# Hybrid decoder trunk on one Trainium2 core: the written order of ScalarE and VectorE in the first group of the up projection

## The chip, the cores and the metric

The kernel runs on one core of one Trainium2 chip. The metric is device time of one execution in microseconds; of the kernel before there are three timed runs, and one more execution that the hardware profiler recorded. Names: PE is TensorE, ACT is ScalarE, DVE is VectorE, POOL is GpSimd, SP issues most DMA transfers.

## The reference

One decoder layer on 1024 tokens of width 1024, all in fp32: RMSNorm, a combined input projection, a pooling mixer beside six heads of a gated recurrence, the output projection with a residual, then the MLP and a last RMSNorm. The change lies in the MLP:

```python
    h2 = rms_norm(x, norm_mlp_g[l])
    x = x + jnp.square(jax.nn.relu(h2 @ w_up[l])) @ w_down[l]     # w_up 1024x4096, w_down 4096x1024
```

## The kernel before, in words

Every fp32 operand of a large product is split into two parts (`split`, L114): ACT writes `hi`, a rounded copy; DVE writes `lo = src - hi`. `mm3` (L119) then issues three matmuls: hi by hi (L122), hi by lo (L123), lo by hi (L124). So no product of the MLP starts before ACT and DVE have both touched both of its operands.

The up projection runs in eight groups of 512 columns of `w_up`. Each group is a 2x2 block product by a scheme of seven block products instead of eight. `h2`, the normed and transposed input, lies in four quarters `quad[dk, half]` (half of the 1024 rows of `w_up`, half of the tokens); a group's weights lie in four blocks `raw_wu_{g}_{fh}{dk}`. The token side of product n is `h2op_n`, made once in the first group and used by all eight; the weight side `whi_wu_{g}_n`, `wlo_wu_{g}_n` is made anew in each group. Sums and differences of quarters and blocks (`mixed_blocks` L738, `up_weights` L789: `wsum`, `wdif`) are DVE's.

One product is 24 matmuls of 512 columns into two PSUM banks (e = 0, 1). Products 1, 6, 7 and 4 accumulate one after another in the banks `ps_ua`, 5 and 3 in `ps_uc`, 2 in `ps_ub`. Between two products that share a bank pair the partial sum has to be drained into SBUF (`sums_out` L866): ACT copies it out after products 1, 5 and 6, DVE adds it to an earlier sum after 2, 3 and 7. The next product on that bank waits for the drain. The drains go to tiles `hid` that take the place of quarters no longer needed: the first takes the place of `quad[0,0]`, the source of `h2op_6`, so it waits until both parts of `h2op_6` are made. Finished quarters of the hidden layer are sent to DRAM by POOL's DMA queue (`keep` L863).

The first group runs its products in the order 1, 2, 5, 6, 3, 7, 4 (the others 1, 5, 6, 3, 7, 2, 4). It overlaps the end of the stage before it: the transposes of the last row tile (`mlp_input(7)`, tile `pt_h2_7`) stand on PE between products 1 and 2, and from them ACT and DVE make the last 128 tokens of `h2op_5` and the sources of `h2op_6`, `h2op_3`, `h2op_7` and `h2op_4`.

What sets the order: PE's instructions stand as written. ACT and DVE are ordered by a scheduler, except inside `tc.manual_schedule`, where they stand as written as well. In the kernel before this holds from L829 up to the end of group 0 (L918). In the trace each engine runs its instructions in that order, and what stands behind one that waits is held up with it.

Of the kernel before, what the change touches and what calls it, by code (L numbers as in the profile page):

```python
# [10 lines left out]
F32 = mybir.dt.float32  # L11
F32R = mybir.dt.float32r
# [3 lines left out]
ALU = mybir.AluOpType  # L16
# [44 lines left out]
def kernel(  # L61
# [52 lines left out]
    def split(hi, lo, src):  # L114

        act.copy(hi, src)  # L116
        dve.tensor_tensor(out=lo, in0=src, in1=hi.bitcast(F32), op=ALU.subtract)  # L117
# [540 lines left out]
    def sub(out_, a, b):  # L658
        dve.tensor_tensor(out=out_, in0=a, in1=b, op=ALU.subtract)  # L659
# [11 lines left out]
    with ExitStack() as pb:  # L671
# [63 lines left out]
            h2[n] = pair_of(pool_, f"h2op_{n}")  # L735
            split(*h2[n], src)

        def mixed_blocks(i):  # L738


            b11, b12, b21, b22 = (quad[k][:, :, i % 4 * P:(i % 4 + 1) * P] for k in ((0, 0), (0, 1), (1, 0), (1, 1)))
            sub(b11, b12, b11)
            sub(b12, b22, b12)
            split(*(t[:, :, i % 4 * P:(i % 4 + 1) * P] for t in h2[5]), b11)
            sub(b11, b22, b11)
            sub(b21, b21, b11)

        def product_out(step, dh):
# [37 lines left out]
            nc.sync.dma_start(t, w_up_v[:, 4 * dk:4 * dk + 4, c0:c0 + 256])  # L786
            return t

        def up_weights(g, n, w, s):  # L789

            if n == 5:
                s[0] = sums.tile([P, 4, 256], F32, tag="sum", name=f"wsum_{g}")
                add(s[0], w[1, 0], w[1, 1])
            elif n == 6:
                sub(s[0], s[0], w[0, 0])
            elif n == 3:
                sub(s[0], w[0, 1], s[0])
            elif n == 7:
                s[1] = sums.tile([P, 4, 256], F32, tag="sum", name=f"wdif_{g}")
                sub(s[1], w[0, 0], w[1, 0])  # L800
            src = {1: w[0, 0], 2: w[0, 1], 3: s.get(0), 4: w.get((1, 1)), 5: s.get(0), 6: s.get(0), 7: s.get(1)}[n]
            pool_ = wring["split"][0]
            hi = pool_.tile([P, 4, 256], F32R, tag="whi", name=f"whi_wu_{g}_{n}")
            lo = pool_.tile([P, 4, 256], F32R, tag="wlo", name=f"wlo_wu_{g}_{n}")
            split(hi, lo, src)
            return hi, lo

# [18 lines left out]
            w_first[fh, dk] = up_raw(0, fh, dk, pool_)  # L826
        for n in (1, 2, 5):
            split_first[n] = up_weights(0, n, w_first, s_first)
        steady = tc.manual_schedule(engines={mybir.EngineType.DVE, mybir.EngineType.Activation})  # L829
        steady.__enter__()  # L830
        for n, key in ((1, "a"), (2, "b")):
            first[key] = up_banks(0, key)
            for _ in up_product(n, split_first[n], first[key], True):
                pass
            if n == 1:
                split_first[6] = up_weights(0, 6, w_first, s_first)
                mlp_input(7)
                mixed_blocks(7)

        later = {6: (big, quad[0, 0]), 3: (big, quad[1, 1]), 7: (big2, quad[0, 1]), 4: (big2, quad[1, 0])}  # L840

        def up_group(g, order):
            if g:
                w = {(fh, dk): up_raw(g, fh, dk, pool_) for fh, dk, pool_ in ((0, 0, wraw), (0, 1, wraw), (1, 0, rawp), (1, 1, rawp))}
                banks, s, ready = {}, {}, {}
            else:
                w, banks, s, ready = w_first, dict(first), s_first, split_first
# [30 lines left out]
                    if e:  # L878
                        relu2(c[q])

            for at_, n in enumerate(order):
                key = {1: "a", 6: "a", 7: "a", 4: "a", 5: "c", 3: "c", 2: "b"}[n]
                if g == 0:
                    for m in order[3:at_ + 3] or order[3:4]:
                        if m in later:
                            operand(m, *later.pop(m))
                            if m not in ready:
                                ready[m] = up_weights(g, m, w, s)
                if g == 0 and n in (1, 2):
                    for e in range(2):  # L890
                        sums_out(n, e, banks[key][e])
                else:
                    fresh = key not in banks
                    if fresh:
                        banks[key] = up_banks(g, key)
                    weights = ready[n] if n in ready else up_weights(g, n, w, s)
                    for e in up_product(n, weights, banks[key], fresh):
                        sums_out(n, e, banks[key][e])
                if n in (2, 7, 4):
                    keep({2: 1, 7: 4, 4: 2}[n], c[{2: 11, 7: 22, 4: 21}[n]])  # L900
                if n == order[-2]:

                    s3 = quarter("hs3")
                    sub(s3, c[11], c[12])
                    keep(7, s3)
                    add(c[12], c[12], c[22])
                    keep(5, c[12])
                    s2 = quarter("hs2")
                    sub(s2, c[12], c[11])
                    keep(6, s2)  # L910
# [3 lines left out]

        for g in range(UP_GROUPS):
            up_group(g, ORDER if g else FIRST_ORDER)
            if g == 0:
                steady.__exit__(None, None, None)  # L918
    quadp.release()
    sums.release()  # L920
    rawp.release()
# [178 lines left out]
```

## Time and profile before

| | us |
|---|---|
| median of 3 runs | 1112.06 (1111.24 to 1114.28) |
| the profiled execution | 1111.47 |
| its span, first to last instruction | 1109.7 |
| PE busy in the span | 1084.5 (98%) |
| DVE busy | 792.5 (71%) |
| ACT busy | 422.2 (38%) |

The span is divided into 40 slices of 27.7 us. Shares of busy time are means over stages that have different limits; matmuls are pipelined, so a busy PE counts a slow matmul as busy too. PEclk is the clock granted to TensorE, 1.00 or 9 tenths and more being 2.4 GHz and half of it 1.2 GHz; a mean in between says that part of the stretch ran at either. In a timeline a row is one instruction or several equal ones; what stands in brackets is the engine's idle time before it and what ended that.

### The profile page before, as it was taken

The numbers are of one execution on the slowest core, as the hardware profiler recorded it, in microseconds if no ns is written. First come the engines' busy times: TensorE is split into PE (matmuls) and PEld (weight loads), VectorE is DVE, ScalarE is ACT, GpSimd is POOL, SyncE is SP. The second block draws the span as 40 slices with busy tenths as digits, with TensorE's granted clock in tenths as the row PEclk, the third lists the DMA queues.
The fourth block names the chain that finished last, engine by engine and source line by source line (L and its number), as shares of the span: only waits on it lengthen the run. The fifth ranks groups of instructions, "written<-read, shape, count | busy, mean of one in ns | idle before, by whom it ended". The sixth has DMA issues, their size and how long they took to land.

```text
span 1109.7 us, 14274 instructions
## 1 busy us (share of the span) xinstructions
PE 1084.5 (98%) x5728; PEld 896.0 (81%) x5728; DVE 792.5 (71%) x1068; ACT 422.2 (38%) x647; POOL 81.9 (7%) x124
## 2 busy tenths in 40 slices
PE   8989999999999999997999999999999999999996
PEld 6868797879787788876888888888888888888885
DVE  4398847784779852688678558756988978777774
ACT  6744333434332522344332233233344424233343
POOL 1001010101010111100010011001000000000001
PEclk9999999999999999998999999999999999999998
DMA  9421011110110162313544354336994344344104
GB/s 318 148 58 38 21 39 38 39 39 20 58 39 19 58 218 95 105 39 108 176 177 146 114 190 171 133 114 221 368 354 185 124 180 161 113 164 177 38 1 152
DMA packets 71362, 137.55 MB, mean 124 GB/s; under 512 B 4864, under 2 KB 44928, under 8 KB 67712
## 3 DMA queue, kind: packets, MB, share of 16 engines
q1 hardware_dynamic: 60656, 100.98, 26.8%
q0 software_dynamic: 9344, 33.56, 7.8%
q10 hardware_dynamic: 1296, 2.10, 0.5%
q8 instruction: 45, 0.74, 0.3%
q14 instruction: 21, 0.17, 0.0%
HBM read 98.87 MB, written 37.75 MB: 123 GB/s over the span
## 4 chain that ended last, share of the span: by engine, by line
PE 80%; DVE 11%; issue 3%; ACT 3%; DMA 2%; POOL 1%; SPq 0%; ACTq 0%; POOLq 0%; DVEq 0%
PE ps_dx L123 5%; PE ps_dx L124 5%; PE ps_dx L122 5%; PE ps_ua L122 5%; PE ps_ua L124 5%; PE ps_ua L123 5%; PE ps_dy L123 3%; PE ps_dy L124 3%; PE ps_dy L122 3%; PE ps_uc L124 2%; PE ps_uc L122 2%; PE ps_uc L123 2%; PE ps_o L122 2%; PE ps_o L124 2%; PE ps_o L123 2%
## 5 line engine op out<-in xcount | busy, mean ns | idle before, releaser
L116 ACT CAST wdop<-raw_wd 128x2048 fp32r<-128x2048 f32 x28 | 53.6, 1913 | 155.6 <-PE ps_dy L124 49.1
L122 PE MATMUL ps_ua<-h2op,whi_wu 128*128 128x512 f32 x256 | 100.5, 393 | 3.9 <-DVE hid L662 3.8
L124 PE MATMUL ps_ua<-h2op,wlo_wu 128*128 128x512 f32 x256 | 100.5, 392 | 0.0
L123 PE MATMUL ps_ua<-h2op,whi_wu 128*128 128x512 f32 x256 | 100.2, 392 | 0.0
L122 PE MATMUL ps_dx<-wdop,hop 128*128 128x512 f32 x256 | 99.6, 389 | 0.0
L123 PE MATMUL ps_dx<-wdop,hop 128*128 128x512 f32 x256 | 99.6, 389 | 0.0
L124 PE MATMUL ps_dx<-wdop,hop 128*128 128x512 f32 x256 | 99.6, 389 | 0.0
L117 DVE TENSOR_TENSOR wdop<-raw_wd,wdop 128x2048 fp32r<-128x2048 f32 x28 | 64.1, 2290 | 28.7 <-ACT wdop L116 28.7
L117 DVE TENSOR_TENSOR wlo_wu<-raw_wu,whi_wu 128x1024 fp32r<-128x1024 f32 x24 | 29.2, 1222 | 52.9 <-ACT whi_wu L116 52.9
L117 DVE TENSOR_TENSOR hop<-hraw,hop 128x2048 fp32r<-128x2048 f32 x28 | 64.0, 2284 | 3.4 <-ACT hop L116 3.4
L116 ACT CAST hop<-hraw 128x2048 fp32r<-128x2048 f32 x28 | 53.4, 1910 | 32.1 <-DMA hraw<-hid 20.8
L116 ACT CAST whi_wu<-wsum 128x1024 fp32r<-128x1024 f32 x24 | 25.3, 1053 | 96.7 <-DVE wsum L659 41.2
L122 PEld LDWEIGHTS ps_ua<-h2op,whi_wu 128*128 128x128 f32 x256 | 48.5, 189 | 14.7 <-issue 4.2
L662 DVE TENSOR_TENSOR x<-ps_dx,x 128x512 f32<-128x512 f32 x64 | 43.9, 688 | 20.3 <-PE ps_dx L124 20.3
L124 PEld LDWEIGHTS ps_ua<-h2op,wlo_wu 128*128 128x128 f32 x256 | 48.4, 189 | 10.5 <-DVE wlo_wu L117 0.4
L123 PEld LDWEIGHTS ps_ua<-h2op,whi_wu 128*128 128x128 f32 x256 | 48.5, 189 | 10.2
L122 PE MATMUL ps_v<-whi_v,hT_hi 128*128 128x256 f32 x192 | 54.5, 285 | 1.8 <-ACT whi_v L116 1.8
L122 PEld LDWEIGHTS ps_dx<-wdop,hop 128*128 128x128 f32 x256 | 48.1, 188 | 10.0
L123 PEld LDWEIGHTS ps_dx<-wdop,hop 128*128 128x128 f32 x256 | 48.1, 188 | 9.9
L124 PEld LDWEIGHTS ps_dx<-wdop,hop 128*128 128x128 f32 x256 | 48.1, 188 | 9.9
L123 PE MATMUL ps_v<-wlo_v,hT_hi 128*128 128x256 f32 x192 | 54.3, 284 | 0.8 <-DVE wlo_v L117 0.8
L124 PE MATMUL ps_v<-whi_v,hT_lo 128*128 128x256 f32 x192 | 54.1, 284 | 0.0
(234 smaller groups left out, 2781.2 us busy)
## 6 DMA issues: line engine op xcount, KB each, us to landing
hid<-hid POOLq DMA_DIRECT2D x56, 512.0 KB, 3.1
hraw<-hid SPq DMA_DIRECT2D x28, 1024.0 KB, 5.0
raw_wu<-in_w_up_dram SPq DMA_DIRECT2D x32, 512.0 KB, 3.7
raw_wd<-in_w_down_dram SPq DMA_DIRECT2D x16, 1024.0 KB, 7.1
xt<-in_x_t_dram SPq DMA_DIRECT2D x8, 512.0 KB, 7.5
xn<-in_x_dram SPq DMA_DIRECT2D x8, 512.0 KB, 6.9
x<-x_mid SPq DMA_DIRECT2D x8, 512.0 KB, 6.0
raw_v<-in_w_in_dram SPq DMA_DIRECT2D x6, 512.0 KB, 3.9
```

What stands on the lines that cost most here:

```text
L116: act.copy(hi, src)
L117: dve.tensor_tensor(out=lo, in0=src, in1=hi.bitcast(F32), op=ALU.subtract)
L122: pe.matmul(ps, lh, rh, start=start, stop=False, skip_group_check=goes_on)
L123: pe.matmul(ps, lh, rl, start=False, stop=False, skip_group_check=goes_on)
L124: pe.matmul(ps, ll, rh, start=False, stop=stop, skip_group_check=goes_on)
L662: dve.tensor_tensor(out=out_, in0=a, in1=b, op=ALU.add)
```

## The change

Only group 0 is written anew; the groups after it keep their code, and PE keeps its order. `split` is taken apart into `hi_part` (ACT) and `lo_part` (DVE), and the two are written at different places. The manual order now begins before the bank pair of product 1 is taken and ends after the operands of product 4, so the drains of 3, 7 and 4 in group 0 are placed by the scheduler.

```diff
--- before.py
+++ after.py
@@ -735,14 +735,23 @@
             h2[n] = pair_of(pool_, f"h2op_{n}")
             split(*h2[n], src)
 
-        def mixed_blocks(i):
+        def hi_part(hi, lo, src):
+            act.copy(hi, src)
+
+        def lo_part(hi, lo, src):
+            dve.tensor_tensor(out=lo, in0=src, in1=hi.bitcast(F32), op=ALU.subtract)
+
+        def mixed_blocks(i, between=lambda: None):
 
 
             b11, b12, b21, b22 = (quad[k][:, :, i % 4 * P:(i % 4 + 1) * P] for k in ((0, 0), (0, 1), (1, 0), (1, 1)))
             sub(b11, b12, b11)
+            part = *(t[:, :, i % 4 * P:(i % 4 + 1) * P] for t in h2[5]), b11
+            hi_part(*part)
+            between()
+            lo_part(*part)
+            sub(b11, b22, b11)
             sub(b12, b22, b12)
-            split(*(t[:, :, i % 4 * P:(i % 4 + 1) * P] for t in h2[5]), b11)
-            sub(b11, b22, b11)
             sub(b21, b21, b11)
 
         def product_out(step, dh):
@@ -786,7 +795,7 @@
             nc.sync.dma_start(t, w_up_v[:, 4 * dk:4 * dk + 4, c0:c0 + 256])
             return t
 
-        def up_weights(g, n, w, s):
+        def up_sum(g, n, w, s):
 
             if n == 5:
                 s[0] = sums.tile([P, 4, 256], F32, tag="sum", name=f"wsum_{g}")
@@ -798,10 +807,15 @@
             elif n == 7:
                 s[1] = sums.tile([P, 4, 256], F32, tag="sum", name=f"wdif_{g}")
                 sub(s[1], w[0, 0], w[1, 0])
-            src = {1: w[0, 0], 2: w[0, 1], 3: s.get(0), 4: w.get((1, 1)), 5: s.get(0), 6: s.get(0), 7: s.get(1)}[n]
+            return {1: w[0, 0], 2: w[0, 1], 3: s.get(0), 4: w.get((1, 1)), 5: s.get(0), 6: s.get(0), 7: s.get(1)}[n]
+
+        def up_split(g, n):
             pool_ = wring["split"][0]
-            hi = pool_.tile([P, 4, 256], F32R, tag="whi", name=f"whi_wu_{g}_{n}")
-            lo = pool_.tile([P, 4, 256], F32R, tag="wlo", name=f"wlo_wu_{g}_{n}")
+            return tuple(pool_.tile([P, 4, 256], F32R, tag=f"w{part}", name=f"w{part}_wu_{g}_{n}") for part in ("hi", "lo"))
+
+        def up_weights(g, n, w, s):
+            src = up_sum(g, n, w, s)
+            hi, lo = up_split(g, n)
             split(hi, lo, src)
             return hi, lo
 
@@ -826,20 +840,40 @@
             w_first[fh, dk] = up_raw(0, fh, dk, pool_)
         for n in (1, 2, 5):
             split_first[n] = up_weights(0, n, w_first, s_first)
-        steady = tc.manual_schedule(engines={mybir.EngineType.DVE, mybir.EngineType.Activation})
-        steady.__enter__()
-        for n, key in ((1, "a"), (2, "b")):
-            first[key] = up_banks(0, key)
-            for _ in up_product(n, split_first[n], first[key], True):
-                pass
-            if n == 1:
-                split_first[6] = up_weights(0, 6, w_first, s_first)
-                mlp_input(7)
-                mixed_blocks(7)
-
-        later = {6: (big, quad[0, 0]), 3: (big, quad[1, 1]), 7: (big2, quad[0, 1]), 4: (big2, quad[1, 0])}
+        places_first = {6: (big, quad[0, 0]), 3: (big, quad[1, 1]), 7: (big2, quad[0, 1]), 4: (big2, quad[1, 0])}
+
+        def first_operand(n):
+            pool_, src = places_first[n]
+            h2[n] = pair_of(pool_, f"h2op_{n}")
+            return *h2[n], src
+
+        def first_weights(n):
+            src = up_sum(0, n, w_first, s_first)
+            split_first[n] = up_split(0, n)
+            return *split_first[n], src
+
+
+        in_order = tc.manual_schedule(engines={mybir.EngineType.DVE, mybir.EngineType.Activation})
+        in_order.__enter__()
+        first["a"] = up_banks(0, "a")
+        for _ in up_product(1, split_first[1], first["a"], True):
+            pass
+        mlp_input(7)
+        made = {}
+        mixed_blocks(7, lambda: made.update({6: first_weights(6)}))
+        made["op6"] = first_operand(6)
+        hi_part(*made[6])
+        hi_part(*made["op6"])
+        lo_part(*made[6])
+        lo_part(*made["op6"])
+        made["op3"] = first_operand(3)
+        hi_part(*made["op3"])
+        first["b"] = up_banks(0, "b")
+        for _ in up_product(2, split_first[2], first["b"], True):
+            pass
 
         def up_group(g, order):
+
             if g:
                 w = {(fh, dk): up_raw(g, fh, dk, pool_) for fh, dk, pool_ in ((0, 0, wraw), (0, 1, wraw), (1, 0, rawp), (1, 1, rawp))}
                 banks, s, ready = {}, {}, {}
@@ -878,24 +912,46 @@
                     if e:
                         relu2(c[q])
 
-            for at_, n in enumerate(order):
-                key = {1: "a", 6: "a", 7: "a", 4: "a", 5: "c", 3: "c", 2: "b"}[n]
-                if g == 0:
-                    for m in order[3:at_ + 3] or order[3:4]:
-                        if m in later:
-                            operand(m, *later.pop(m))
-                            if m not in ready:
-                                ready[m] = up_weights(g, m, w, s)
-                if g == 0 and n in (1, 2):
-                    for e in range(2):
-                        sums_out(n, e, banks[key][e])
-                else:
-                    fresh = key not in banks
-                    if fresh:
-                        banks[key] = up_banks(g, key)
-                    weights = ready[n] if n in ready else up_weights(g, n, w, s)
-                    for e in up_product(n, weights, banks[key], fresh):
-                        sums_out(n, e, banks[key][e])
+            def drain(n):
+                for e in range(2):
+                    sums_out(n, e, banks[bank_of[n]][e])
+
+            def run(n):
+                key = bank_of[n]
+                fresh = key not in banks
+                if fresh:
+                    banks[key] = up_banks(g, key)
+                weights = ready[n] if n in ready else up_weights(g, n, w, s)
+                return up_product(n, weights, banks[key], fresh)
+
+            bank_of = {1: "a", 6: "a", 7: "a", 4: "a", 5: "c", 3: "c", 2: "b"}
+            if g == 0:
+                drain(1)
+                made[3] = first_weights(3)
+                lo_part(*made["op3"])
+                for e in run(5):
+                    sums_out(5, e, banks["c"][e])
+                hi_part(*made[3])
+                lo_part(*made[3])
+                made["op7"] = first_operand(7)
+                hi_part(*made["op7"])
+                made[7] = first_weights(7)
+                hi_part(*made[7])
+                drain(2)
+                keep(1, c[11])
+                for e in run(6):
+                    sums_out(6, e, banks["a"][e])
+                lo_part(*made["op7"])
+                lo_part(*made[7])
+                made["op4"], made[4] = first_operand(4), first_weights(4)
+                for part in (hi_part, lo_part):
+                    part(*made["op4"])
+                    part(*made[4])
+                in_order.__exit__(None, None, None)
+                order = order[4:]
+            for n in order:
+                for e in run(n):
+                    sums_out(n, e, banks[bank_of[n]][e])
                 if n in (2, 7, 4):
                     keep({2: 1, 7: 4, 4: 2}[n], c[{2: 11, 7: 22, 4: 21}[n]])
                 if n == order[-2]:
@@ -914,8 +970,6 @@
 
         for g in range(UP_GROUPS):
             up_group(g, ORDER if g else FIRST_ORDER)
-            if g == 0:
-                steady.__exit__(None, None, None)
     quadp.release()
     sums.release()
     rawp.release()
```

ACT, around the last transposes. `quad` rows are the copies of the transposed tile, `h2op` and `whi_wu` are `hi` parts (`whi_wu_0_6` is group 0, product 6), `hid` rows are drains. Before:

```order
L116 CAST whi_wu_0_5_4391<-wsum_0_4389 128x1024
L116 CAST whi_wu_0_6_4424<-wsum_0_4389 128x1024
L730 COPY quad_01_3700<-pt_h2_7_0_4428 128x4x128
L730 COPY quad_11_3703<-pt_h2_7_1_4434 128x4x128
L116 CAST h2op_5_4179<-quad_00_3702 128x4x128
L116 CAST h2op_6_4472<-quad_00_3702 128x2048
L872 COPY hid_0_0_4475<-ps_ua_0_0_4397 128x512
L872 COPY hid_0_0_4475<-ps_ua_0_1_4398 128x512
L116 CAST h2op_3_4482<-quad_11_3703 128x2048
L116 CAST whi_wu_0_3_4486<-wsum_0_4389 128x1024
```

After:

```order
L116 CAST whi_wu_0_5_4391<-wsum_0_4389 128x1024
L730 COPY quad_01_3700<-pt_h2_7_0_4423 128x4x128
L730 COPY quad_11_3703<-pt_h2_7_1_4429 128x4x128
L739 CAST h2op_5_4179<-quad_00_3702 128x4x128
L739 CAST whi_wu_0_6_4438<-wsum_0_4389 128x1024
L739 CAST h2op_6_4444<-quad_00_3702 128x2048
L739 CAST h2op_3_4449<-quad_11_3703 128x2048
L906 COPY hid_0_0_4477<-ps_ua_0_0_4397 128x512
L906 COPY hid_0_0_4477<-ps_ua_0_1_4398 128x512
L906 COPY hid_0_0_4477<-ps_uc_0_0_4484 128x512
L906 COPY hid_0_0_4477<-ps_uc_0_1_4485 128x512
L739 CAST whi_wu_0_3_4481<-wsum_0_4389 128x1024
```

The two copies of the transposes and the last part of `h2op_5` now stand ahead of `whi_wu_0_6`; `h2op_3` stands ahead of the drain of product 1; and the drain of product 5 stands ahead of `whi_wu_0_3`.

DVE, from the `lo` part of `h2op_6` to that of product 7's weights (`ps_ub` is product 2's drain, the row behind its two is the squared ReLU). Before:

```order
L117 TENSOR_TENSOR h2op_6_4472<-quad_00_3702,h2op_6_4472 128x2048
L662 TENSOR_TENSOR hid_0_0_4475<-ps_ub_0_0_4446,hid_0_0_4475 128x512
L662 TENSOR_TENSOR hid_0_0_4475<-ps_ub_0_1_4447,hid_0_0_4475 128x512
L861 SCALAR_TENSOR_TENSOR hid_0_0_4475<-hid_0_0_4475 128x1024
L117 TENSOR_TENSOR h2op_3_4482<-quad_11_3703,h2op_3_4482 128x2048
L659 TENSOR_TENSOR wsum_0_4389<-raw_wu_0_01_4375,wsum_0_4389 128x1024
L117 TENSOR_TENSOR wlo_wu_0_3_4487<-wsum_0_4389,whi_wu_0_3_4486 128x1024
L117 TENSOR_TENSOR h2op_7_4518<-quad_01_3700,h2op_7_4518 128x2048
L659 TENSOR_TENSOR wdif_0_4521<-raw_wu_0_00_4373,raw_wu_0_10_4377 128x1024
L117 TENSOR_TENSOR wlo_wu_0_7_4524<-wdif_0_4521,whi_wu_0_7_4523 128x1024
```

After:

```order
L742 TENSOR_TENSOR h2op_6_4444<-quad_00_3702,h2op_6_4444 128x2048
L659 TENSOR_TENSOR wsum_0_4389<-raw_wu_0_01_4375,wsum_0_4389 128x1024
L742 TENSOR_TENSOR h2op_3_4449<-quad_11_3703,h2op_3_4449 128x2048
L742 TENSOR_TENSOR wlo_wu_0_3_4482<-wsum_0_4389,whi_wu_0_3_4481 128x1024
L659 TENSOR_TENSOR wdif_0_4516<-raw_wu_0_00_4373,raw_wu_0_10_4377 128x1024
L662 TENSOR_TENSOR hid_0_0_4477<-ps_ub_0_0_4451,hid_0_0_4477 128x512
L662 TENSOR_TENSOR hid_0_0_4477<-ps_ub_0_1_4452,hid_0_0_4477 128x512
L895 SCALAR_TENSOR_TENSOR hid_0_0_4477<-hid_0_0_4477 128x1024
L742 TENSOR_TENSOR h2op_7_4514<-quad_01_3700,h2op_7_4514 128x2048
L742 TENSOR_TENSOR wlo_wu_0_7_4519<-wdif_0_4516,whi_wu_0_7_4518 128x1024
```

The three rows of product 2's drain stood directly behind `h2op_6` and stand now behind the operands of product 3.

DVE, from the operands of product 4 to the drain of product 7 (`ps_ua`); `ps_uc` is the drain of product 3, `wlo_wu_1_1` belongs to group 1. Before:

```order
L117 TENSOR_TENSOR h2op_4_4554<-quad_10_3701,h2op_4_4554 128x2048
L117 TENSOR_TENSOR wlo_wu_0_4_4558<-raw_wu_0_11_4379,whi_wu_0_4_4557 128x1024
L662 TENSOR_TENSOR hid_0_1_4539<-ps_uc_0_0_4490,hid_0_1_4539 128x512
L662 TENSOR_TENSOR hid_0_1_4539<-ps_uc_0_1_4491,hid_0_1_4539 128x512
L117 TENSOR_TENSOR wlo_wu_1_1_4667<-raw_wu_1_00_4656,whi_wu_1_1_4666 128x1024
L861 SCALAR_TENSOR_TENSOR hid_0_1_4539<-hid_0_1_4539 128x1024
L662 TENSOR_TENSOR hid_0_0_4475<-ps_ua_0_0_4397,hid_0_0_4475 128x512
L662 TENSOR_TENSOR hid_0_0_4475<-ps_ua_0_1_4398,hid_0_0_4475 128x512
```

After:

```order
L742 TENSOR_TENSOR h2op_4_4554<-quad_10_3701,h2op_4_4554 128x2048
L742 TENSOR_TENSOR wlo_wu_0_4_4556<-raw_wu_0_11_4379,whi_wu_0_4_4555 128x1024
L662 TENSOR_TENSOR hid_0_1_4537<-ps_uc_0_0_4484,hid_0_1_4537 128x512
L662 TENSOR_TENSOR hid_0_1_4537<-ps_uc_0_1_4485,hid_0_1_4537 128x512
L662 TENSOR_TENSOR hid_0_0_4477<-ps_ua_0_0_4397,hid_0_0_4477 128x512
L895 SCALAR_TENSOR_TENSOR hid_0_1_4537<-hid_0_1_4537 128x1024
L117 TENSOR_TENSOR wlo_wu_1_1_4667<-raw_wu_1_00_4656,whi_wu_1_1_4666 128x1024
L662 TENSOR_TENSOR hid_0_0_4477<-ps_ua_0_1_4398,hid_0_0_4477 128x512
```

The first half of product 7's drain moved up by two rows, ahead of the squared ReLU and `wlo_wu_1_1`; its second half stands behind them.

## Rows read from the trace of the kernel before

**Rows 1.** The page: busy time of each engine; granted clock in 40 slices.

```profile
PE 1084.5 (98%) x5728; PEld 896.0 (81%) x5728; DVE 792.5 (71%) x1068; ACT 422.2 (38%) x647; POOL 81.9 (7%) x124
...
PEclk9999999999999999998999999999999999999998
```

**Rows 2.** Busy time by stretch; columns in the first line.

```profile
core 0: us, PE busy (x) PEld busy (x) DVE busy (x) ACT busy (x) POOL busy (x), PEclk, DMA share, GB/s
478.50:529.20 50.70, 44.37 (x180) 34.26 (x178) 41.94 (x44) 21.78 (x26) 3.33 (x6) 0.93 0.26 88
529.20:567.30 38.10, 38.10 (x170) 31.56 (x169) 28.01 (x29) 12.03 (x15) 3.19 (x6) 1.00 0.49 166
490.60:497.30 6.70, 6.05 (x24) 4.42 (x24) 4.73 (x6) 2.84 (x4) 0.00 (x0) 1.00 0.00 0
504.80:512.30 7.50, 7.45 (x24) 5.67 (x25) 4.83 (x4) 4.00 (x5) 0.00 (x0) 0.77 0.26 70
522.00:529.20 7.20, 7.17 (x25) 5.75 (x25) 7.20 (x7) 1.64 (x2) 1.60 (x3) 0.76 0.37 146
```

**Rows 3.** Timeline of PE in group 0: start, us, instruction [idle before, releaser].

```profile
484.08 1.03 PE L728 MATMUL pt_h<-ident,hn 128*128 128x128 f32 x8
484.87 0.48 PE L122 MATMUL ps_ub<-h2op,whi_wu 128*128 128x512 f32 x1
...
490.96 0.50 PE L122 MATMUL ps_uc<-h2op,whi_wu 128*128 128x512 f32 x1 [0.39 <-ACT h2op L116]
...
497.32 0.50 PE L122 MATMUL ps_ua<-h2op,whi_wu 128*128 128x512 f32 x1
...
504.80 0.50 PE L122 MATMUL ps_uc<-h2op,whi_wu 128*128 128x512 f32 x1 [1.75 <-ACT hid L872]
...
508.32 0.63 PE L122 MATMUL ps_uc<-h2op,whi_wu 128*128 128x512 f32 x1
...
512.35 0.39 PE L122 MATMUL ps_ua<-h2op,whi_wu 128*128 128x512 f32 x1
...
522.03 0.47 PE L122 MATMUL ps_ua<-h2op,whi_wu 128*128 128x512 f32 x1 [3.83 <-DVE hid L662]
...
529.20 0.39 PE L122 MATMUL ps_ua<-h2op,whi_wu 128*128 128x512 f32 x1
```

**Rows 4.** Timeline of ACT in group 0.

```profile
487.34 1.05 ACT L116 CAST whi_wu<-wsum 128x1024 fp32r<-128x1024 f32 x1 [4.80 <-DVE wsum L659]
488.30 1.07 ACT L730 COPY quad<-pt_h 128x512 f32<-128x512 f32 x2
...
492.41 1.91 ACT L116 CAST h2op<-quad 128x2048 fp32r<-128x2048 f32 x1 [1.50 <-DVE quad L659]
496.68 1.07 ACT L872 COPY hid<-ps_ua 128x512 f32<-128x512 f32 x2 [2.36 <-DVE h2op L117]
...
504.17 1.07 ACT L872 COPY hid<-ps_uc 128x512 f32<-128x512 f32 x2
```

**Rows 5.** Timeline of DVE in group 0.

```profile
483.09 0.69 DVE L659 TENSOR_TENSOR quad<-quad,quad 128x512 f32<-128x512 f32 x1
...
504.30 1.23 DVE L117 TENSOR_TENSOR wlo_wu<-wsum,whi_wu 128x1024 fp32r<-128x1024 f32 x1 [1.11 <-ACT whi_wu L116]
507.07 2.29 DVE L117 TENSOR_TENSOR h2op<-quad,h2op 128x2048 fp32r<-128x2048 f32 x1 [1.55 <-ACT h2op L116]
...
517.74 1.28 DVE L662 TENSOR_TENSOR hid<-ps_uc,hid 128x512 f32<-128x512 f32 x2
518.93 1.22 DVE L117 TENSOR_TENSOR wlo_wu<-raw_wu,whi_wu 128x1024 fp32r<-128x1024 f32 x1
520.06 1.22 DVE L861 SCALAR_TENSOR_TENSOR hid<-hid 128x1024 f32<-128x1024 f32 x1
521.20 1.28 DVE L662 TENSOR_TENSOR hid<-ps_ua,hid 128x512 f32<-128x512 f32 x2
```

**Rows 6.** Instructions of the tiles `hid`, 515 to 540 us: landing of their DMAs.

```profile
DMA to landing us min/median/max: 2.9/2.9/3.3
```

## Prediction, made before the changed kernel was run

> **What bounds the kernel now.** I read the page first: PE is busy 98% of the span, DVE 71%, ACT 38%, and the granted clock is full in every slice but the nineteenth and the last [rows 1]. The last is the end of the kernel. The nineteenth, 18 x 27.7 = 499 to 527 us, lies in group 0 of the up projection. Then a table by stretch: group 0 takes 50.70 us from the start of product 1 (478.50) to the start of group 1, and group 1, with the same 168 matmuls, takes 38.10 with PE busy in all of it [rows 2]. So a product at full pace is 38.10/7 = 5.44 us. Group 0 has eight transposes besides (484.08 to 484.87, 0.79 us [rows 3]) and product 1, which also starts behind transposes, takes 484.08 - 478.50 = 5.58, 0.14 over the pace; I allow product 2 another 0.1. Without a wait the group would take 38.10 + 0.79 + 0.24 = 39.13. The rest, 50.70 - 39.13 = 11.57 us, is what any better order of ACT and DVE can win here. I found no other wait of PE worth a term.
>
> Where the 11.57 lie, product by product, from the starts in [rows 3]. Product 2 starts at 484.87 and ends its matmuls near 490.41 (5.44 + 0.1).
> - Product 5 starts at 490.96 and product 6 at 497.32 instead of 490.41 + 5.44 = 495.85: 1.47 lost.
> - Product 3 starts at 504.80 instead of 497.32 + 5.44 = 502.76: 2.04 lost, behind ACT's drain of product 5.
> - Product 3 runs 7.55 us up to 512.35 instead of 5.44: 2.11 lost. The stretch 504.80 to 512.30 has a granted clock of 0.77 [rows 2], so part of it at 1.2 instead of 2.4 GHz; a matmul there lasts 0.63 us instead of 0.39 [rows 3]. PE had idled 1.75 us just before.
> - Product 7 takes 9.68 us up to 522.03 with the wait behind it, 3.83 of them idle: 4.24 lost, waiting for DVE to take product 7 out of its bank.
> - Product 4 runs 7.17 instead of 5.44, clock 0.76: 1.73 lost, again after idling.
> Sum 11.59. The waits make 7.75 of it and the low clock behind the two longest 3.84.
>
> The cause stands in the rows of ACT and DVE. ACT idles 4.80 us before `whi_wu` of product 6, and behind it both copies of the transposes wait although PE made them at 484.08; they go out at 488.30 [rows 3, 4]. All of DVE's work on the last tile follows from these copies. From there ACT and DVE hand each other one operand at a time: ACT waits 1.50 and 2.36 [rows 4], DVE 1.55 for an `h2op` [rows 5]. At the end DVE writes the drain of product 3, `wlo_wu` of group 1 and the ReLU (517.74 to 521.20) before it takes up product 7, which PE had finished near 518 [rows 3, 5].
>
> **The change part by part.** No instruction is added or removed, PE's order stays, and no DMA is issued from a new place in the program; two spills on POOL's queue swap places, and so do two loads of group 2 on SP's. I walk the new order with durations of the trace. On DVE a 512-wide row is followed after 0.60, a 1024-wide one after 1.13, a 2048-wide one after its 2.29 less the same overlap, 2.20 [rows 5]; a result counts 0.09 later. On ACT these steps are 0.49, 0.96 and 1.82 [rows 4]. DVE's first moved instruction starts at 483.09, as before.
> - Copies first. ACT is free at 482.5 (487.34 - 4.80), the first four transposes end near 484.7, so the copies end near 485.8 instead of 489.4: 3.6 earlier. DVE comes to the last tile's difference after four 0.60 steps and one 1.13 at 486.6, it ends at 487.3; ACT's part of `h2op_5` ends at 488.0; DVE's, behind the 1.13 of `wsum`, at 489.1. Product 5 is due at 490.41: 1.3 in hand, its wait is gone.
> - Product 6. Three differences, the `lo` of its weights and of `h2op_6` follow: 3 x 0.60 + 1.13 + 2.20 after 489.0, ended at 494.3; ACT's `hi` of `h2op_6`, which starts behind the first difference, ends at 491.7, just ahead of DVE. ACT's two drains of product 1 wait for that and end at 494.9 and 495.4; due 495.85 and 498.6. 0.9 in hand.
> - Product 3. `wsum`, `h2op_3` (ACT made its `hi` ahead, by 493.6) and `wlo` take 1.13 + 2.20 + 1.13, so up to 498.8. ACT's four drains end when product 5 does, near 496.7, and its `whi` at 497.7, just as DVE wants it. Due 501.3: over 2 in hand. This is the 2.04 wait and, with it, the slow clock behind it.
> - Product 7. `wdif`, product 2's drain (1.19 + 1.13 [rows 5]), `h2op_7`, `wlo`: 1.13 + 2.32 + 2.20 + 1.13 brings DVE to 505.7. Due 506.7 for its first matmul and 0.45 later for `wlo`: some 1.2 in hand. The drain behind the splits costs nothing, for only the spill of that quarter waits for it.
> - Product 4. Its operands end at 509.1, product 3's drain at 510.3, the first half of product 7's at 510.9; PE finishes product 7 at 512.2. The second half, behind ReLU and `wlo_wu_1_1`, ends at 513.8 and is due at 514.9. The 3.83 wait and its slow clock are gone too.
> - What is late next: `wlo` of group 1's product 5. DVE never rests from 483.09 on, and this row now stands behind six 1024-wide and two 512-wide rows: it ends near 523.0, and is due at 523.06 + 0.45 = 523.5. 0.5 in hand, the smallest margin. After it DVE has less to do (28.01 of 38.10 in group 1 [rows 2]) and catches up.
>
> So all 11.57 goes, if DVE keeps its pace. The trace has no stretch in which DVE works 40 us without rest; the nearest is 522.0 to 529.2, busy 7.20 of 7.20 [rows 2]. Bounds: its rows there keep their 1.13 step, which gives no loss; if every instruction that uses the result of the one just before it paid 0.14 more, as many as four on this way make 0.56, at most 0.1 beyond the margin. A wait that small doesn't touch the clock: the stretch with the 0.39 wait before product 5 has 1.00 [rows 2, 3]. A gain above 11.57 is excluded, since group 1's pace is PE's floor. I take 11.6.
>
> One rule speaks against an unbroken DVE. The spills of the hidden layer are issued by POOL, and they must land before group 1's drains can reuse the tiles; they landed in 2.9 to 3.3 us [rows 6] although DVE was busy without a pause in 522.0 to 529.2, where three of them were issued. The Trainium skill (GPSIMD Engine Reference, section Specifications) says that GpSimd's SBUF interfaces are shared with VectorE, with contention against instructions with two SBUF inputs, which nearly all of these are. By that rule the spill of the second quarter, ready near 516, would stall until DVE rests, and the gain would be that of the second rival below; by the row it is 11.6.
>
> **The rivals.**
> - Part of the waits comes back elsewhere. For it: margins of 0.5 and 0.9, and a chain of 39 DVE rows in which one late ACT part shifts all. Against it: each step was made with durations that vary by hundredths. A wait of 0.5 to 1.5 without a change of clock gives 11.6 - 1 = 10.6; one like 1.75 with the clock behind it costs 2.0 + 2.1 = 4.1, so 7.5.
> - The spills stall until DVE rests. That is two 1024-wide rows behind the last one above, 525.3; landed at 525.3 + 3.0 = 528.3, ACT's drain of group 1's product 1 and behind it `whi` of product 6 end near 530.5, due 528.5: 2 us and 2 of clock, gain 7.6. The landing time in [rows 6] speaks against it.
> - The waits aren't made by the order. If drains were slow for another reason, copies that come earlier would only wait longer, and PE would keep the 2.04 and 4.24 and the clock behind them: gain 1.5 at most. Against it: the two long waits end within 0.15 us of the first half of the drain that is named, ACT's at 504.17 + 0.58 and DVE's at 521.20 + 0.69 [rows 3 to 5].
> - Slower: DVE becomes the bound. In the new order ACT and DVE work side by side for 40 us. Were DVE's rows longer for that, each per cent would be 0.4 us; PE starts to wait at 1%, and together with two falls of the clock (3.8) the kernel is slower than before from (11.6 - 3.8)/0.4 = 20%; at 25% it is 2 us slower, 1114. Against it: a 1024-wide row beside a working ACT (504.30) takes 1.23, two beside an idle one (518.93, 520.06) 1.22 [rows 5].
>
> **How the numbers follow.** The profiled execution took 1111.47, which is 1.77 around a span of 1109.7; outside group 0 only a few rows of ACT and DVE in group 1 swap places, so it becomes 1111.47 - 11.6 = 1099.9. The median of the runs lies 0.59 above it: 1112.06 - 11.6 = 1100.5. Chances: forecast 0.76; waits in part elsewhere 0.15 (1101.5 to 1104.6); spills 0.02 (1104.5); order not the cause 0.04 (1110.5); slower 0.03. The range goes from the lowest run shown less the gain and a little spread, 1099.0, to a full new wait with its clock, 1104.6. No change means within 0.3%, 3.3 us, about what a measurement of this kernel can resolve: the first three cases are faster, 0.93; the fourth is the same, 0.04; the last slower, 0.03.
>
> **What would show it.** In the profile after: group 0 from product 1 to group 1 in 39.1 to 39.6 us, clock 1.00 in all of it, no wait of PE above 0.5; the copies of `pt_h` on ACT near 484.7; DVE busy over 95% from 483 to 523; the slice with 8 in the clock row gone. I am wrong if PE still waits for a drain in `ps_ua` or `ps_uc`, if group 1 shows waits that it didn't have, or if group 0 is short and the stages behind it are longer by what it saved.

## The result, and the profile after

The changed kernel takes 1100.26 us (median of 4 runs, 1098.87 to 1101.15), the kernel before 1111.65 beside it (4 runs, 1110.69 to 1114.28): ratio 0.9893, 95% interval 0.9873 to 0.9913. The forecast was 1100.5 in a range of 1099.0 to 1104.6.

The page of the profile after: busy times, and the granted clock in 40 slices.

```profile
PE 1079.2 (98%) x5728; PEld 894.1 (81%) x5728; DVE 791.8 (72%) x1068; ACT 422.0 (38%) x647; POOL 81.9 (7%) x124
...
PEclk9999999999999999999999999999999999999998
```

The counts of instructions are those of [rows 1], and the 8 in the nineteenth slice is gone. The table by stretch, group 0 and then group 1, with the columns of [rows 2]:

```profile
478.82:517.93 39.11, 39.11 (x180) 32.46 (x178) 38.28 (x42) 20.64 (x25) 2.81 (x5) 1.00 0.31 101
517.93:556.01 38.08, 38.08 (x170) 31.54 (x168) 30.81 (x31) 13.03 (x17) 3.72 (x7) 1.00 0.53 179
```

Group 0 takes 39.11 us instead of 50.70, with PE busy in all of it at full clock; group 1 keeps its pace. The span fell from 1109.7 to 1098.4, by 11.3, and group 0 by 11.59: all of the gain is here, and the rest of the kernel is 0.3 longer. The starts of the transposes and of products 2, 5, 6, 3, 7, 4 and then of group 1, on PE after:

```profile
484.40 1.03 PE L728 MATMUL pt_h<-ident,hn 128*128 128x128 f32 x8
485.19 0.48 PE L122 MATMUL ps_ub<-h2op,whi_wu 128*128 128x512 f32 x1
...
490.73 0.39 PE L122 MATMUL ps_uc<-h2op,whi_wu 128*128 128x512 f32 x1
...
496.17 0.39 PE L122 MATMUL ps_ua<-h2op,whi_wu 128*128 128x512 f32 x1
...
501.61 0.39 PE L122 MATMUL ps_uc<-h2op,whi_wu 128*128 128x512 f32 x1
...
507.05 0.39 PE L122 MATMUL ps_ua<-h2op,whi_wu 128*128 128x512 f32 x1
...
512.49 0.39 PE L122 MATMUL ps_ua<-h2op,whi_wu 128*128 128x512 f32 x1
...
517.93 0.39 PE L122 MATMUL ps_ua<-h2op,whi_wu 128*128 128x512 f32 x1
```

No row has a wait, and the steps are 5.44 us from product 5 on. The three waits and the slow matmul of [rows 3] are gone. ACT after, where [rows 4] had the wait of 4.80:

```profile
485.04 1.07 ACT L730 COPY quad<-pt_h 128x512 f32<-128x512 f32 x2 [2.16 <-PE pt_h L728]
...
490.15 3.73 ACT L739 CAST h2op<-quad 128x2048 fp32r<-128x2048 f32 x2 [0.27 <-DVE quad L659]
494.70 1.08 ACT L906 COPY hid<-ps_ua 128x512 f32<-128x512 f32 x2 [0.81 <-DVE h2op L742]
495.66 1.30 ACT L906 COPY hid<-ps_uc 128x512 f32<-128x512 f32 x2
496.85 1.05 ACT L739 CAST whi_wu<-wsum 128x1024 fp32r<-128x1024 f32 x1
```

The copies wait for PE's transposes alone, two `h2op` his follow each other (x2), and both drains of product 5 come ahead of `whi` of product 3. DVE after, the rows that the walk dated:

```profile
497.93 1.22 DVE L742 TENSOR_TENSOR wlo_wu<-wsum,whi_wu 128x1024 fp32r<-128x1024 f32 x1
...
504.87 1.22 DVE L742 TENSOR_TENSOR wlo_wu<-wdif,whi_wu 128x1024 fp32r<-128x1024 f32 x1
...
513.41 0.68 DVE L662 TENSOR_TENSOR hid<-ps_ua,hid 128x512 f32<-128x512 f32 x1
...
522.02 1.22 DVE L117 TENSOR_TENSOR wlo_wu<-wsum,whi_wu 128x1024 fp32r<-128x1024 f32 x1
```

They end at 499.15, 506.09, 514.09 and 523.24; the walk had 498.8, 505.7, 513.8 and 523.0. Group 0 also started 0.32 later than before (478.82 against 478.50), so each step is within 0.1 of its forecast.

### The profile page after: what moved, and what is told of

Read it like the earlier page. It is cut to its first block, busy times and chain, and to the rows that moved or that the text cites. A ratio compares the mean times of both kernels' runs of the same rounds, so it can differ in the third digit from the quotient of the medians.

```text
span 1098.4 us, 14269 instructions
## 1 busy us (share of the span) xinstructions
PE 1079.2 (98%) x5728; PEld 894.1 (81%) x5728; DVE 791.8 (72%) x1068; ACT 422.0 (38%) x647; POOL 81.9 (7%) x124
## 4 chain that ended last, share of the span: by engine, by line
PE 85%; DVE 8%; issue 2%; DMA 2%; ACT 2%; POOL 1%; SPq 0%; ACTq 0%; POOLq 0%
PE ps_dx L123 5%; PE ps_ua L124 5%; PE ps_ua L122 5%; PE ps_dx L124 5%; PE ps_dx L122 5%; PE ps_ua L123 5%; PE ps_o L122 3%; PE ps_dy L123 3%; PE ps_uc L124 3%; PE ps_uc L122 3%; PE ps_dy L124 3%; PE ps_dy L122 3%; PE ps_uc L123 3%; PE ps_o L123 3%; PE ps_o L124 3%
```

## Experiments: undoing one part, doing one part

The forecast walked the whole order. It did not show which part carries the gain. Times compare by the ratio to the kernel before in the same series, and by group 0's length in the profile, from product 1's start to group 1's: 50.70 before, 39.11 after.

**Copies late again.** On ACT and DVE, against the changed kernel:

```
+        made = {6: first_weights(6)}
+        hi_part(*made[6])
         mlp_input(7)
-        made = {}
-        mixed_blocks(7, lambda: made.update({6: first_weights(6)}))
+        lo_part(*made[6])
+        mixed_blocks(7)
...
```

> The changed kernel, but the two copies of the last transposes stand behind whi of product 6 on ACT again (and wlo of product 6 ahead of the last tile's differences on DVE). My theory, that PE waits where a row of ACT or DVE ends later than PE wants it, and that the parts of the change each keep a margin: product 5 waits 1.0 to 1.6 us and product 6 another 1.0, nothing behind them; group 0 takes 41.7 instead of 39.1 us, the kernel 1102.9; if the clock falls behind the first wait, up to 2 more, 1104.9. Rival, that this one place was the cause and the rest follows from it: the waits before products 3 and 4 come back with their low clock, 1108 to 1111.

1102.25 us, ratio 0.9917 (0.9904 to 0.9931). PE waits 1.06 and 0.22 in product 5, which starts 1.2 late; product 6 comes another 0.9 late, and the profile marks no wait behind that. Group 0 takes 41.32, 2.2 more than after, clock 1.00. The first theory holds, with 0.4 less than it said. The waits before products 3, 7 and 4 don't come back, so late copies alone don't make them.

**Product 2's drain at once.** `drain(2)` moves from behind the splits to right behind `drain(1)`.

> The changed kernel, but DVE's drain of product 2 (two additions and the ReLU, 2.3 us) stands right behind ACT's drain of product 1, ahead of the splits for products 3 and 7. My theory: product 7 alone waits, 0.8 us, since the drain holds DVE until PE has finished product 2; the kernel takes 1101.1. Rival, that drains ahead of splits were the main cause of the waits: a wait of over 2 us and a low clock behind it, 1104 or more.

1100.60 us, ratio 0.9903 (0.9889 to 0.9916): not to be told from the changed kernel. Group 0 takes 39.55, product 7 starts 0.44 late. The expected reason was wrong: PE had long finished product 2, and DVE waits 0.65 for ACT's copy of product 1 into the same `hid`.

**ACT's lead taken away, in part.** `hi` of `h2op_3` goes behind `drain(1)`, `hi_part(*made[3])` ahead of the drain of product 5.

> The changed kernel, but ACT is not one operand ahead: the hi part of h2op_3 stands behind the drain of product 1, and whi of product 3 ahead of the drain of product 5. My theory: DVE waits about 1.5 us for h2op_3 once and this reaches PE only before product 4, 1.2 us; the kernel takes 1101.5. Rival, that ACT one operand ahead is what breaks the hand-over of pairs: waits before products 3 and 4 both, 1104 to 1108. Second rival, copies first alone was enough: no wait, 1100.3.

1100.71 us, ratio 0.9906 (0.9892 to 0.9921). Group 0 takes 39.92, 0.8 more; the wait (0.34, for `wlo`) shows in product 7, not before product 4. I first read this as: the lead is worth little. It was not fully taken away, though, since the sum for product 3's weights still stood ahead of the `lo` of `h2op_3`.

**Copies first alone.** The kernel before with the copies first; in the same run the sum of product 6's weights (`between`, in `mixed_blocks`) stands behind all of the last tile's differences, where the change has it between the two parts of `h2op_5`:

```
             sub(b21, b21, b11)
+            between()
...
             if n == 1:
-                split_first[6] = up_weights(0, 6, w_first, s_first)
                 mlp_input(7)
-                mixed_blocks(7)
+                mixed_blocks(7, lambda: split_first.update({6: up_weights(0, 6, w_first, s_first)}))
```

> The kernel before, with one part of the change alone: the copies of the last transposes stand ahead of whi of product 6 on ACT, and wlo of product 6 behind the last tile's differences on DVE. My theory: the wait before product 5 goes, but ACT and DVE still hand each other one operand at a time and DVE still drains product 3 ahead of product 7; products 6, 3, 7 and 4 start where they did within 1 us, group 0 takes 50 to 51 us, the kernel 1111 to 1112. Rival, that the late copies were the cause of what follows: 3.6 us or more are won, 1108 or less.

1113.50 us, ratio 1.0013 (1.0003 to 1.0022): slightly slower than before. Its PE timeline at products 5, 6, 3, 7, 4:

```profile
490.19 0.39 PE L122 MATMUL ps_uc<-h2op,whi_wu 128*128 128x512 f32 x1
...
497.44 0.50 PE L122 MATMUL ps_ua<-h2op,whi_wu 128*128 128x512 f32 x1 [1.65 <-ACT hid L872]
...
504.92 0.50 PE L122 MATMUL ps_uc<-h2op,whi_wu 128*128 128x512 f32 x1 [1.73 <-ACT hid L872]
...
512.23 0.50 PE L122 MATMUL ps_ua<-h2op,whi_wu 128*128 128x512 f32 x1 [1.25 <-ACT hid L872]
...
522.14 0.77 PE L122 MATMUL ps_ua<-h2op,whi_wu 128*128 128x512 f32 x1 [3.85 <-DVE hid L662]
```

The wait before product 5 is gone, and PE loses as much before product 6: counted from product 1, products 6, 3, 7 and 4 start within 0.4 us of [rows 3], and product 4 takes 8.12 instead of 7.17. The loss comes from the place of the sum. DVE comes late to the sum for product 6, and ACT's `whi` waits for it, with `hi` of `h2op_6` behind:

```profile
490.33 1.22 DVE L659 TENSOR_TENSOR wsum<-wsum,raw_wu 128x1024 f32<-128x1024 f32 x1
```

```profile
491.58 1.05 ACT L116 CAST whi_wu<-wsum 128x1024 fp32r<-128x1024 f32 x1 [3.82 <-DVE wsum L659]
492.54 1.90 ACT L116 CAST h2op<-quad 128x2048 fp32r<-128x2048 f32 x1
```

Counted from product 1, this `hi` starts at 14.26 here, at 13.91 in [rows 4] and at 11.33 in the changed kernel. So the run does not show what early copies are worth with the sum where the change puts it; the two runs with pairs, below, do. The Trainium skill (Perfetto Trace Analysis, section Optimization Strategy) advises to find the engine's gaps and to make what they wait for start sooner. Done here for the first gap alone, with a sum that came later in exchange, it won nothing.

**Is the low clock a price?** The kernel before with PE kept busy in its waits; the lines are those of the second run, and the first has `4: 0`:

```
+                    for k in range({3: 14, 4: 32}.get(n, 0) if g == 0 else 0):
+                        pe.transpose(spare[0][:, k % 4 * P:(k % 4 + 1) * P], ident, ident)
                     for e in up_product(n, weights, banks[key], fresh):
```

> The kernel before, with 14 transposes of a constant matrix (1.4 us, their result is not used) put on PE ahead of product 3, in the wait of 1.75 us, so that PE does not idle there. The prediction's term: the clock stays full, product 3 takes 5.44 instead of 7.55 us, and the kernel is 2.1 us faster, 1109.5. The rival that the trace of before suggests on a second reading: product 7 waits for DVE's wlo, which ends at 512.84 in any case, so the low clock of product 3 turns into a wait of about 2 us ahead of product 7; the kernel stays at 1111.6, and the clock may fall behind that wait.

1112.18 us, ratio 1.0004 (0.9994 to 1.0015). The transposes and the starts of products 3, 7 and 4 in its PE timeline:

```profile
501.80 1.69 PE L900 MATMUL pt_h<-ident 128*128 128x128 f32 x14
503.69 0.50 PE L122 MATMUL ps_uc<-h2op,whi_wu 128*128 128x512 f32 x1 [0.20 <-ACT hid L874]
...
511.01 0.50 PE L122 MATMUL ps_ua<-h2op,whi_wu 128*128 128x512 f32 x1 [1.26 <-ACT hid L874]
...
520.92 0.77 PE L122 MATMUL ps_ua<-h2op,whi_wu 128*128 128x512 f32 x1 [3.85 <-DVE hid L662]
```

Product 3 runs at clock 1.00, and product 7 still starts 7.32 us behind it (7.55 in [rows 3]): the low clock became a wait, as the rival said. Product 4 starts 43.54 us behind product 1, and 43.53 before the change. So the prediction's 2.11 was no price of the clock. Product 4 itself takes 8.09 here instead of 7.17, at clock 0.66, and group 0 is 0.9 longer for it. Products 3 and 4, in columns as in [rows 2]:

```profile
503.70:511.00 7.30, 6.01 (x24) 4.34 (x24) 4.63 (x4) 3.81 (x5) 0.00 (x0) 1.00 0.25 71
520.90:529.00 8.10, 8.08 (x24) 6.47 (x25) 8.10 (x8) 1.64 (x2) 1.60 (x3) 0.66 0.40 159
```

> The kernel before, with such transposes of a constant matrix (results not used) ahead of product 3 (14) and ahead of product 4 (32, 3.2 us, in the wait of 3.83). The prediction's terms: both low clocks go, 2.11 + 1.73 = 3.8 us faster, 1107.8. The rival: only the second is a price of its own, 1.7 us faster, 1109.9. A third way, that the clock falls behind another wait or in spite of the transposes: 1111.6.

1109.97 us, ratio 0.9985 (0.9976 to 0.9994). With 32 more transposes ahead of it, product 4 runs at 1.00 in 5.56 us; group 0 takes 49.11, 1.59 less than before. Product 4:

```profile
522.40:528.00 5.60, 5.53 (x24) 4.62 (x25) 5.60 (x6) 1.65 (x2) 1.07 (x2) 1.00 0.24 91
```

The second term, 1.73, was real.

**Pairs again.** What sets 7.3 us, then? The changed kernel with the operands of products 3 and 7 made one after the other, as before the change:

```
                 drain(1)
+                made["op3"] = first_operand(3)
+                hi_part(*made["op3"])
+                lo_part(*made["op3"])
                 made[3] = first_weights(3)
-                lo_part(*made["op3"])
+                hi_part(*made[3])
+                lo_part(*made[3])
                 for e in run(5):
                     sums_out(5, e, banks["c"][e])
...
```

> The changed kernel, but the operands of products 3 and 7 are made pair by pair again: hi and lo of h2op, only then the weights' sum, their hi and lo, and ACT's drain of product 5 behind whi of product 3. Copies first and product 2's drain behind the splits stay. My theory now, after the run in which ACT's lead alone was taken away cost little: the sum of the weights ahead of the operand's lo is what frees ACT, because whi waits for the sum and the drain of product 5 waits behind whi in ACT's queue. Waits of about 1.6 us before product 3 (for that drain), 2.0 before product 7 and 2.8 before product 4; 6.4 in all, 1106.7, and up to 1108.4 with a low clock behind the last. Rival, that ACT's lead is worth no more than that run showed: 1100.3 to 1101.5.

1107.48 us, ratio 0.9949 (0.9937 to 0.9962). Waits of 0.87, 1.25 and 2.27 before products 3, 7 and 4, and product 4 at clock 0.76; by the starts products 3, 7 and 4 come 1.0, then another 1.9 and another 2.9 late, and product 4 takes 1.7 more. Group 0 takes 46.62, 7.5 more than after. Its DVE timeline, from one `h2op` lo to the next:

```profile
498.59 2.29 DVE L742 TENSOR_TENSOR h2op<-quad,h2op 128x2048 fp32r<-128x2048 f32 x1 [2.95 <-ACT h2op L739]
500.80 1.22 DVE L659 TENSOR_TENSOR wsum<-raw_wu,wsum 128x1024 f32<-128x1024 f32 x1
503.13 1.23 DVE L742 TENSOR_TENSOR wlo_wu<-wsum,whi_wu 128x1024 fp32r<-128x1024 f32 x1 [1.11 <-ACT whi_wu L739]
505.91 2.29 DVE L742 TENSOR_TENSOR h2op<-quad,h2op 128x2048 fp32r<-128x2048 f32 x1 [1.55 <-ACT h2op L739]
```

And ACT in the same run, between the same two:

```profile
502.05 1.05 ACT L739 CAST whi_wu<-wsum 128x1024 fp32r<-128x1024 f32 x1 [3.50 <-DVE wsum L659]
503.00 1.07 ACT L904 COPY hid<-ps_uc 128x512 f32<-128x512 f32 x2
503.96 1.91 ACT L739 CAST h2op<-quad 128x2048 fp32r<-128x2048 f32 x1
```

This is the clockwork: lo of `h2op` (DVE), sum (DVE), `whi` (ACT), `wlo` (DVE) beside the drains, then the next `h2op` hi (ACT), and around again: 505.91 - 498.59 = 7.32 us a product. PE needs 5.44. Product 5 had ended at 497.16, but its drain goes out at 503.00, since it stands behind `whi` in ACT's queue, `whi` waits for the sum, and the sum stands behind the 2.29 us row of DVE. With the sum ahead of the lo and ACT's his early, DVE has neither of its two idles (1.11 + 1.55) in the cycle.

**Pairs and late copies.** Both at once; of the change only the drains' places are left.

> As the run with pairs again, and the copies of the last transposes behind whi of product 6 as well; of the change only the drains' places stay. My theory: waits before products 5, 6, 3, 7 and 4 as in the kernel before, 9.3 us in all, 1109.6 to 1111.3, so that the drains' places alone win at most 2 us. Rival, that the drains' places carry the gain: 1106 or less.

1109.16 us, ratio 0.9968 (0.9955 to 0.9980); group 0 takes 47.91, with waits of 0.99, 1.57, 1.26 and 2.27, and product 4 this time at clock 1.00. That is 2.79 less than before the change, where at most 2 was expected: product 4 starts 1.16 sooner, and the other 1.63 is its full clock, which no run shows to come from the drains' places. The starts of products 6 and 4, in the run with pairs again and then in this one:

```profile
497.16 0.39 PE L122 MATMUL ps_ua<-h2op,whi_wu 128*128 128x512 f32 x1
...
519.28 0.69 PE L122 MATMUL ps_ua<-h2op,whi_wu 128*128 128x512 f32 x1 [2.27 <-DVE hid L662]
```

```profile
498.02 0.50 PE L122 MATMUL ps_ua<-h2op,whi_wu 128*128 128x512 f32 x1
...
520.98 0.47 PE L122 MATMUL ps_ua<-h2op,whi_wu 128*128 128x512 f32 x1 [2.27 <-DVE hid L662]
```

Counted from product 1 (479.82 and 478.61), product 6 starts at 17.34 and 19.41, product 4 at 39.46 and 42.37. Only the order around the last tile differs. So the early copies are kept through the slow cycle: everything from product 3 on comes 2.9 us sooner, and the cycle stays at 7.32. Up to 0.6 of this is not the copies, since the sum of product 6's weights starts 8.14 behind product 1 here and 7.53 in the kernel before. The medians are only 1.7 apart because product 4 runs at the lower clock in the run with pairs again.

**ACT's lead alone.** Copies late, product 2's drain at once, the written order kept to the end of group 0; only the sums and ACT's his stay ahead.

> The changed kernel with everything undone but ACT's lead and the sums ahead of the los: copies behind whi of product 6, product 2's drain at once, the written order kept until the end of group 0, so that the drains of products 3 and 7 stand where it puts them. My theory: against the kernel before the waits ahead of products 3 and 4 shrink; 6 us slower than the changed kernel, 1106.2, and up to 1108 with a low clock behind the wait before product 4 (about 2.2): one part alone gives back 4 to 5.5 of the 11.6. Rival, that no part alone wins anything, as copies first alone did not: 1111 to 1112.

1106.82 us, ratio 0.9950 (0.9936 to 0.9963): this part alone gives back about half, 6.05 of 11.59 in group 0. Waits of 1.00 (product 5), 0.64 (`wlo` in product 3) and 1.88 (before product 4), clock 1.00, group 0 44.65. No run moves the sums alone; that they weigh more than ACT's lead is only suggested, by the run with the lead taken away in part (0.8) against pairs again (5.8 without its clock).

**The written order to the end of group 0.**

```
-                in_order.__exit__(None, None, None)
...
+            if g == 0:
+                in_order.__exit__(None, None, None)
```

> The changed kernel, but the written order of ACT and VectorE holds until the end of group 0, so that the drains of products 3, 7 and 4 stand where it puts them and not where the scheduler does. My theory: the operand rows come as in the changed kernel; the drain of product 7 stands behind a ReLU and product 4 waits 1.5 us for it: 1101.8, or up to 1103.5 if the clock falls behind that wait. Rival, that the places of these drains take no part: 1100.3.

1102.82 us, ratio 0.9907 (0.9894 to 0.9921). Product 4 waits 1.00 for the drain of product 7; group 0 takes 40.36, 1.25 more than after, at full clock.

**How near DVE is to its limit.** Rows added at the end of the written order:

```
                     part(*made[4])
+                for _ in range(1):
+                    lo_part(*made[4])
```

> The changed kernel with one 1024-wide VectorE row more in group 0 (wlo of product 4 is written twice, 1.13 us). My theory: VectorE has no rest from 482 to 525 us, and the smallest margin of a row that PE wants is 0.5 us, so PE waits 0.4 to 0.6 us in all, before product 4 or group 1's product 5; the kernel takes 1100.7. Rival, that VectorE still had room in group 0: no wait.

1101.94 us in one run, in which group 0 starts 1.64 us later than in the profile after, so the time says little here. Group 0 takes 39.25, only 0.14 more, and the profile marks no wait. That is less than expected: DVE has no rest, but the scheduler, which places the later rows, put `wdif` behind the `wlo` that was the tightest, and so made room for the row.

> The changed kernel with three 1024-wide VectorE rows more in group 0 (wlo of product 4 is written four times, 3.4 us). My theory: each row behind the margin costs its full 1.13, so PE waits 2.9 to 3.8 us, nearly all before product 4, and such a wait brings the clock down as in before: 1103.1 to 1104.1 at full clock, 1105 to 1106 with a low clock of 1.7 to 2.1 us. Rival, that VectorE had room: 1100.3 to 1101.

1105.08 us, ratio 0.9946 (0.9926 to 0.9967), with `range(3)`. PE waits 3.27 before product 4, which then runs 7.13 us at clock 0.76:

```profile
515.41 0.47 PE L122 MATMUL ps_ua<-h2op,whi_wu 128*128 128x512 f32 x1 [3.27 <-DVE hid L662]
```

Group 0 takes 44.19, 5.1 more than after: 3.4 of waits and slips, which is the three rows of 1.13, and 1.7 of clock. So DVE has about one row's room at this place in group 0, not three.

## Why the prediction was right, point by point

- The sum. The 11.57 above the floor of 39.13 went entirely; group 0 fell by 11.59. This held because the floor came from group 1, which has the same matmuls, and did not need the causes of the single waits.
- The walk. The dates came within about 0.1 us of the trace, because ACT and DVE did the same rows with the same durations: in a stretch of over 40 us without rest a 1024-wide row of DVE still took 1.22. The price of 0.14 for back-to-back rows, and the slower case built on it, did not show.
- "The waits make 7.75 of it and the low clock behind the two longest 3.84." This split was wrong, though the sum was not. The 2.11 at product 3 was no price of the clock: at full clock the same time became a wait (1.0004). The 1.73 at product 4 was one (0.9985). The sum did not depend on the split, since the changed order took both away; that is why the forecast came out in spite of it.
- The cause. "Behind it both copies wait ... All of DVE's work on the last tile follows from these copies" is a real part and the smaller one: late copies cost 2.2 in group 0 of the changed kernel and 2.9 in the starts beside the pairs, and with early copies the waits before products 3, 7 and 4 still stand (0.87, 1.25 and 2.27). "From there ACT and DVE hand each other one operand at a time" named the larger part, without its number: a cycle of 7.32 us against PE's 5.44. Undoing this alone cost 7.5, and this alone gave back half. Undone one at a time, the parts cost 2.2, 7.5, 1.25 and 0.4 in group 0, together 11.4. That this comes near the whole is partly chance: the 7.5 holds 1.7 of a low clock that was not there in the run with pairs and late copies.
- Drains behind splits. Costed at nothing; undone, 0.44 in group 0. Where the scheduler rather than the written order places the last drains, 1.25 is won, which the prediction had inside its 4.24.
- The smallest margin, 0.5 before group 1's product 5, measured 0.58 (`wlo` ends at 523.24, due at 523.37 + 0.45). It is no hard limit, as the run with one row more shows.
- The spills. The instructions of the tiles `hid`, 495 to 530 us, after:

```profile
DMA to landing us min/median/max: 3.0/3.9/4.3
```

In [rows 6] it was 2.9/2.9/3.3. Those issued between 515.53 and 518.93 landed in 3.0 to 3.5 us, while DVE had no pause before 525.5, so they did not stall until it rests; the slowest of all took 1 us longer than in [rows 6]. The Trainium skill (GPSIMD Engine Reference, section Specifications) has the shared SBUF interfaces as a point of contention. The trace fits a small price of that kind and does not show its cause; that such a spill would wait until DVE rests was the prediction's own reading. No drain waited for it.

## What to carry to other kernels

Where two engines hand one operand to and fro for a third, add up one whole cycle of the hand-over, waits included, and compare it with the third engine's time per step. If the cycle is longer, a faster third engine does not help (product 3 at full clock only waited more), and an earlier start is won once (2.9 us here) and leaves the cycle as long as it was. What shortens the cycle is work of one engine taken out of it, here sums and his one operand ahead. When one part is tried alone, check in the trace that nothing else has moved: the run with copies first alone also made a sum later, and lost by it what the copies won. And before a low clock is charged as a loss, ask whether what comes next was waiting for something else anyway; filler work in the wait tells.

## What the runs showed of the hardware

Whether the clock falls behind a wait can't be told from the wait's length alone. Product 4 behind 2.27 us, in the run with pairs again and then in that with pairs and late copies:

```profile
519.20:526.40 7.20, 7.12 (x24) 5.75 (x25) 7.20 (x7) 0.60 (x1) 1.60 (x3) 0.76 0.58 216
```

```profile
520.90:526.50 5.60, 5.52 (x24) 4.62 (x25) 5.60 (x6) 0.60 (x1) 1.07 (x2) 1.00 0.53 183
```

The granted clock, the third number from the end, tells the two apart: 0.76, part of it at 1.2 GHz, and 1.00, all at 2.4. So too product 3 behind 1.75 us before (0.77) and behind 1.73 with copies first alone (1.00). After 3.27 to 3.85 us it fell each time, and product 4 then cost 1.7 to 2.7 us more than 5.44: 0.76 in the kernel before and with three rows more, 0.65 and 0.66 with copies first alone and with PE busy ahead of product 3. What else decides stays open, so behind a wait of about 2 us a term for the clock belongs in the range rather than in the sum.
